# A two-layer hybrid mixer step on one core: early column groups cut into steps of two chunks, x scaled ahead, GpSimd relieved of a power and of transfers

## The chip, the cores and the metric

The kernel runs on one core of a Trainium2 chip. The metric is the device time of one execution in microseconds, of which the median over several runs is given. The engines are named as the profile names them: PE (matrix products; PEld loads its weights), DVE (vector), ACT (scalar functions), POOL (GpSimd) and SP (the engine that issues most transfers).

## The reference

The reference is one step of a network with two layers over 128 context tokens and 256 latent tokens, each a vector of 2048 numbers. A layer makes a shift, a scale and a gate from a conditioning vector (one for each kind of token), normalises the tokens, projects them to 7184 columns, runs four branches on the columns, and projects back:

```python
mod = jax.nn.silu(cond) @ lp['ada_w'] + lp['ada_b']
shift, scale, gate = jnp.split(mod, 3, axis=-1)
xm = rmsnorm(x, lp['norm_w']) * (1.0 + scale) + shift
pr = split_projection(xm @ lp['w_in'])
...
y = jnp.concatenate([out_a, out_b, out_c, out_d], axis=-1) @ lp['w_out']
x = x + gate * y
```

`out_a` is a gated linear recurrence in both directions, `out_b` a neighbourhood attention, `out_c` a grouped-query attention whose queries and keys are divided by their root mean square per head (`rmsnorm(pr['gqa_q'], ...)`) and rotated, and `out_d` a matrix memory (mLSTM). A last `rmsnorm` follows both layers. Besides the tokens, the new keys, values and branch states are written out.

## The kernel before

Tokens lie along the free axis: `xh[k]` and `xl[k]`, k from 0 to 15, hold chunk k of the modulated input, 128 features by 384 tokens (T), as a high and a low part, which together keep fp32 precision. A weight step loads two chunks' rows of up to 512 columns (`raw`), ACT rounds them to `wh`, POOL subtracts to get `wl` (`w_split`), and PE adds three products per chunk and block of output (`block`, the matmuls of line 1361): high by high, high by low, low by high. Blocks of 128 columns are numbered `nb`.

The modulation matrix `ada_w` is far larger than what PE could take beside its own work, so DVE computes it. `ada_dve` queues, for each half `s` of the matrix columns that serves two chunks, 16 rows of pieces: each piece multiplies a 128x512 tile (`araw`) by a condition and adds it to a sum in PSUM (`sbp`; line 196 as seen through the helper `stt`). Two transposes and two reductions (line 347, tile `red`) close the half. Then `ada_final` has PE pick the row sums (line 301, a matmul called the **selector** below), and a few small DVE operations put shift and scale for chunks 2s and 2s+1 into `mod` and `Amul`. Half 0 is made by PE at the start (`ada_pe`). Halves 8 to 11 are the gate. A selector stands in PE's queue at a fixed place: PE does nothing behind it until DVE has finished the half.

With shift and scale there, `modulate` makes `xh` and `xl` of a chunk: a product on DVE (`xmt`), a rounding with the shift on ACT (`xh`), the remainder on DVE (`xl`), each for the 128 context and the 256 latent tokens apart.

So that PE can start before all halves are there, the first layer visits nine column ranges (`E0`: `vif` to `gqa_k`, 4112 columns) in groups of chunks. `KG[0]` gives the chunks of each group: the plan runs all nine ranges over the group, then the next group. Between groups, the sum of a range is parked in SBUF: for `nb` 0 to 2 ACT copies it back to PSUM and out again (`PREB`), for `nb` 3 DVE adds. The late ranges (`ml_gate`, `na_k` and so on) run over all 16 chunks once. `merge` and the `due` list spread the pieces between weight steps. The lists give the order in which the code is written; the framework then sets each engine's queue, which is fixed when the kernel runs.

In the attention branch `br_gqa`, ACT sums the squares of 18 heads, POOL raises them to the power -1/2 (line 981), and DVE multiplies queries and keys (line 196), after which POOL issues the transfer of the keys (line 988) and DVE rotates them (lines 999 to 1004). PE transposes the result (line 1012), and ACT copies it to `gqT` and `gkT`.

Of the kernel before, what the change touches and what calls it, by code (L numbers as in the profile page):

```python
# [9 lines left out]
F32 = mybir.dt.float32  # L10
F32R = mybir.dt.float32r
# [66 lines left out]
def tile_hybrid_step(ctx: ExitStack, tc: tile.TileContext, I, O):  # L78
# [18 lines left out]
    E0 = ["vif", "ml_q", "ml_k", "ml_o", "lru_gate", "ml_v", "lru_x", "na_q", "gqa_k"]  # L97
    L0 = ["ml_gate"]
    NCRIT = 4
    SPREAD_AT, NPART = 2, 3  # L100
    YS = (4.0, 2.5, 1.0, 0.1)
    PRE = {0: True, 1: False}
    KG = {0: [2, 2, 2, 2, 4, 4], 1: [8, 8]}
    START = "PxPPxPPxPPxrPDDwwDD"
# [324 lines left out]
    def modulate(l, k, segs=((0, 0, TP), (1, TP, T))):  # L429
        if l == 0:  # L430
            x = xr[k]
        elif k < KG[1][0]:
            x = X[:, k, :]
        else:
            xr[k] = big.tile([128, T], F32, name=f"xr{k}", tag=f"xl{k}", bufs=1)
            if k < 14:
                nc.sync.dma_start(xr[k], xdram[:, k, :])
                x = xr[k]
            else:
                nc.sync.dma_start(xr[k].rearrange("p (t n) -> p t n", t=3), xtmd[:, :, (k - 14) * 128:(k - 13) * 128])  # L440
                x = from_tm(k)
        t = wrk.tile([128, T], F32, name="xmt", tag="t15", bufs=4)
        for c, a, b in segs:
            stt(t[:, a:b], x[:, a:b], Amul[:, l, k, c:c + 1], rbc[:, a:b], OP.mult, OP.mult)
        for c, a, b in segs:
            act(xh[k][:, a:b], t[:, a:b], AF.Identity, bias=mod[:, l, k, c:c + 1])
        if l == 0 or KG[1][0] <= k:
            xl[k] = big.tile([128, T], F32R, name=f"xl{k}", tag=f"xl{k}", bufs=1)
        for c, a, b in segs:
            stt(xl[k][:, a:b], t[:, a:b], mod[:, l, k, c:c + 1], xh[k].bitcast(F32)[:, a:b],  # L450
                OP.add, OP.subtract)

    def split_cat(k):
# [73 lines left out]
    def lru_alloc(key):  # L527
        t = six(key)
        v = lru_pad(t)
        nc.gpsimd.memset(v[:, :, 0:1], 0.0)  # L530
        nc.gpsimd.memset(v[:, :, 129:132], 0.0)
        nc.gpsimd.memset(v[:, :, 388:390], 0.0)
        return t

# [24 lines left out]
    kv_get = lazy("gqa_kv", lambda t: t[:, 0:1536].rearrange("p (s t n) -> p s t n", s=2, t=3), six)  # L559
    if_get = lazy("ml_if", lambda t: t, lambda key: wts.tile([128, 3, 16], F32, name="ml_if", tag="ml_if", bufs=1))  # L560
    gv_get = lazy("gqa_v", lambda t: t, lambda key: wts.tile([128, 3, 256], F32, name="gqa_v", tag="gqa_v", bufs=1))

# [67 lines left out]
    def br_mlstm(l):  # L630
# [33 lines left out]
        for h in range(4):  # L664
# [123 lines left out]
            yield 1.0  # L788
        nc.gpsimd.dma_start(O["mm"][l:l + 1, :], mnew)


    def br_lru(l):
# [29 lines left out]
        for g in range(4):  # L822
# [45 lines left out]
            yield 4.0  # L868
        nc.gpsimd.dma_start(O["lru"][l], lout)

# [92 lines left out]
    def br_gqa(l):  # L963
# [13 lines left out]
        for t in range(3):  # L977
            for ap, i, _ in heads(t):
                act(junk, ap, AF.Square, accum=ss[:, i:i + 1])
        nc.vector.tensor_scalar(ss, ss, 1.0 / 128, EPS, op0=OP.mult, op1=OP.add)  # L980
        nc.gpsimd.tensor_tensor(ss, ss, rpow[:, 0:18], op=OP.pow)  # L981
        ssq = ss.rearrange("p (t h) -> p t h", t=3)[:, :, 0:4]
        nc.vector.tensor_scalar(ssq, ssq, SC, None, op0=OP.mult)
        yield 8.0
        for t in range(3):
            for ap, i, wn in heads(t):
                stt(ap, ap, ss[:, i:i + 1], wn, OP.mult, OP.mult)
        nc.gpsimd.dma_start(O["gqa_k"][l], kk[:, 0, :])
        yield 2.0
        for t in range(2):  # L990
            cos = gqk[:, t * 128:(t + 1) * 128]
            sin = gqk[:, 256 + t * 128:256 + (t + 1) * 128]
            for ap, nh, wi in ((gq[:, 1 + t, :], 4, 0), (kk[:, 1 + t, :], 2, 1)):
# [10 lines left out]
                nc.vector.tensor_add(ap, ap, rot)  # L1004
            yield 4.0
        qT = cm(six("gqT"))
        kT = cm(six("gkT"))
# [48 lines left out]
    def lru_pairs(nb, ps):  # L1056
        return [(lru_get()[:, nb, 1:129], ps[:, 0:TP]), (lru_get()[:, nb, 132:388], ps[:, TP:T])]

    G = {
        "vif": tm_group([("gqa_v", 256), ("ml_if", 16)],  # L1060
                        lambda nb, ps: [(gv_get()[:, nb, :], ps[:, 0:256]), (if_get()[:, nb, :], ps[:, 256:272])]),
        "ml_q": cm_group("ml_q", lazy("ml_q", lambda t: t, lambda key: cat[:, 8:12, :]), SC),
# [3 lines left out]
                         start(br_mlstm)),  # L1066
        "lru_x": ("cm", [("lru_x", 512)], lru_pairs, copy_out(lru_pairs, 1.0, start(br_lru))),
        "na_q": cm_group("na_q", lazy("na_q", cm, six), SC),
# [104 lines left out]
    for l in range(DEPTH):  # L1173
# [6 lines left out]
        for i in range(len(KG[l])):  # L1180
            if i:
                side += ada_ss(l, kb[i], kb[i + 1]) + [mod_item(l, kb[i], kb[i + 1])]
                due.append((len(main) - LAG, len(side)))
            main += visits(l, EARLY[l], kb[i], kb[i + 1])
        m = o = 0
# [322 lines left out]
    for tok in START:  # L1508
# [5 lines left out]
        elif tok == "w":  # L1514
            upto("w", wl, w_dma, pos["w"] + 1)
        elif tok == "r":
            rstd_bc()
        elif tok == "P":
            it = first.pop(0)
            a_dma(it)  # L1520
            ada_pe(it)
        elif tok == "D":
            it = a_items[pos["a"]]
            upto("a", a_items, a_dma, pos["a"] + 1)
            ada_dve(it)
            it["early"] = True
# [154 lines left out]
```

## Time and profile before

| what | value |
|---|---|
| median of 3 runs | 1498.09 us (1495.1 to 1500.49) |
| the profiled execution | 1499.25 us |
| its span from first to last instruction | 1497.5 us |
| mean granted clock of PE | 0.975 |
| PE, DVE, ACT, POOL busy | 1411.3, 1083.7, 791.6, 922.0 us |

The profile is of one execution. Between its span and its time lie 1.75 us outside the instructions. A busy share is an average over stages: what an edit is worth is read from the stage in which it lies.

### The profile page before, as it was taken

To read this page: it belongs to the slowest core of one execution; us is meant where nothing else is said; L and a number is where in the kernel's file an instruction comes from. 1 tells how busy PE (TensorE), PEld (TensorE's weight loads), DVE (VectorE), ACT (ScalarE), POOL (GpSimd) and SP (SyncE) were. 2 spreads that over 40 slices of the span, in tenths; PEclk is the share of its full clock that TensorE was granted. 3 is DMA by queue.
4 is the path that set the end of the run, shared out by engine and by line. 5 is a ranking of instruction groups with operands and counts; after the bars stand their busy time and mean duration, and the time that the engine had idled before them with its cause. 6 is when DMAs were issued, how large, how long until landed. Compare 5 with 4: busy or idle time off the path is not lost. (4 is left out here: it accounts for less than half of the span.)

```text
span 1497.5 us, 23805 instructions
## 1 busy us (share of the span) xinstructions
PE 1411.3 (94%) x7999; PEld 1329.8 (89%) x7999; DVE 1083.7 (72%) x2053; ACT 791.6 (53%) x1609; POOL 922.0 (62%) x1230
## 2 busy tenths in 40 slices
PE   5989959999999899799998999999999999899997
PEld 1989949989998799799998999999999879899997
DVE  4989999989699956675658999646749761753533
ACT  4689936656445767353334334333454777463432
POOL 1656627666656774845646665766566875855762
PEclk8999979999999999999999999999999999999999
DMA  8877768776568555465747887655456444355433
GB/s 282 265 245 228 230 190 246 228 214 196 155 186 269 163 145 155 160 199 175 259 129 248 267 256 225 180 152 149 142 154 205 142 143 120 97 195 169 139 125 97
DMA packets 167164, 281.68 MB, mean 188 GB/s; under 512 B 17216, under 2 KB 48960, under 8 KB 166912
## 3 DMA queue, kind: packets, MB, share of 16 engines
q1 hardware_dynamic: 159520, 272.40, 59.6%
q10 hardware_dynamic: 7296, 7.48, 1.5%
q8 instruction: 62, 1.02, 0.3%
q14 instruction: 62, 0.51, 0.1%
q0 software_dynamic: 224, 0.27, 0.1%
HBM read 271.17 MB, written 8.93 MB: 187 GB/s over the span
## 5 line engine op out<-in xcount | busy, mean ns | idle before, releaser
L1243 POOL TENSOR_TENSOR wl<-raw,wh 128x256 fp32r<-128x256 f32 (+1 forms) x1152 | 874.5, 792 | 525.8 <-ACT wh L192 440.5
L1361 PE MATMUL acc<-xh,wh 128*128 128x384 f32 x1636 | 568.3, 348 | 15.4 <-ACT xh L192 7.0
L1361 PE MATMUL acc<-xh,wl 128*128 128x384 f32 x1636 | 553.0, 338 | 3.5 <-POOL wl L1243 3.5
L1361 PE MATMUL acc<-xl,wh 128*128 128x384 f32 x1636 | 555.0, 339 | 0.0
L196 DVE SCALAR_TENSOR_TENSOR sbp<-araw,pers,sbp 128x512 f32<-128x512 f32 x690 | 518.4, 751 | 20.9 <-DMA araw<-in_ada_n 8.1
L192 ACT ACTIVATE wh<-raw 128x1024 fp32r<-128x1024 f32 (+2 forms) x304 | 307.0, 1012 | 345.6 <-PE acc L1361 254.8
L1361 PEld LDWEIGHTS acc<-xh,wh 128*128 128x128 f32 x1636 | 309.3, 189 | 21.7 <-ACT xh L192 7.6
L1361 PEld LDWEIGHTS acc<-xh,wl 128*128 128x128 f32 x1636 | 309.2, 189 | 4.8 <-POOL wl L1243 4.8
L1361 PEld LDWEIGHTS acc<-xl,wh 128*128 128x128 f32 x1636 | 309.6, 189 | 1.4
L1361 PE MATMUL acc<-wh,xl 128*128 128x512 f32 (+2 forms) x454 | 166.6, 367 | 5.8 <-DVE xl L196 4.5
L1361 PE MATMUL acc<-wh,xh 128*128 128x512 f32 (+2 forms) x454 | 162.7, 359 | 0.0
L1361 PE MATMUL acc<-wl,xh 128*128 128x512 f32 (+2 forms) x454 | 161.7, 357 | 0.0
L1361 PEld LDWEIGHTS acc<-wh,xl 128*128 128x128 f32 x454 | 87.4, 193 | 21.8 <-DVE xl L196 7.8
L1361 PEld LDWEIGHTS acc<-wl,xh 128*128 128x128 f32 x454 | 87.2, 192 | 12.8
L1361 PEld LDWEIGHTS acc<-wh,xh 128*128 128x128 f32 x454 | 87.5, 193 | 10.9
L196 DVE SCALAR_TENSOR_TENSOR cat<-acc,pers,xold 128x128 f32<-128x128 f32 (+1 forms) x56 | 20.5, 410 | 65.7 <-PE acc L1361 65.7
L192 ACT ACTIVATE xh<-xmt,pers 128x128 fp32r<-128x128 f32 x72 | 29.4, 430 | 43.0 <-DVE xmt L196 42.9
L192 ACT ACTIVATE cat<-acc 128x384 f32<-128x384 f32 (+1 forms) x78 | 38.1, 498 | 8.8 <-PE acc L1361 7.8
L196 DVE SCALAR_TENSOR_TENSOR xl<-xmt,pers,xh 128x128 fp32r<-128x128 f32 x72 | 39.4, 567 | 2.1 <-ACT xh L192 1.9
L388 DVE TENSOR_TENSOR arena<-arena,sq 128x384 f32<-128x384 f32 x38 | 25.9, 682 | 17.4 <-ACT sq L192 16.0
L1361 PE MATMUL s<-xh,wh 128*128 128x384 f32 x92 | 32.2, 350 | 4.4 <-ACT xh L192 3.7
L192 ACT ACTIVATE xh<-cat 128x384 fp32r<-128x384 f32 x32 | 16.5, 519 | 37.1 <-PE acc L1361 19.6
(339 smaller groups left out, 1778.1 us busy)
## 6 DMA issues: line engine op xcount, KB each, us to landing
raw<-in_w_in SPq DMA_DIRECT2D x208, 512.0 KB, 4.0
araw<-in_ada_n SPq DMA_DIRECT2D x368, 256.0 KB, 4.3
raw<-in_w_out SPq DMA_DIRECT2D x64, 512.0 KB, 4.0
raw<-in_w_in SPq DMA_DIRECT2D x32, 256.0 KB, 3.1
araw<-in_ada_n SPq DMA_DIRECT2D x8, 512.0 KB, 5.3
xr<-in_xT SPq DMA_DIRECT2D x16, 192.0 KB, 5.2
nac<-in_nac SPq DMA_DIRECT2D x8, 288.0 KB, 4.4
xold<-in_xT SPq DMA_DIRECT2D x3, 768.0 KB, 6.1
```

The costliest lines, as they stand in the source:

```text
L192: return nc.scalar.activation(out, in_, f, bias=bias, scale=scale)
L196: return nc.vector.scalar_tensor_tensor(out, a, s, b, op0=op0, op1=op1)
L388: eng.tensor_tensor(sqacc, sqacc, s, op=OP.add)
L1243: nc.gpsimd.tensor_tensor(it["lo"][:, kk, cs], raw[:, kk, cs], hv[:, kk, cs], op=OP.subtract)
L1361: last_ev["pe"] = nc.tensor.matmul(out, a, b, start=s0 and i == 0, stop=s1 and i == 2, skip_group_check=not it["first"]).ins
```

## The change

`KG[0]` goes from groups of 2, 2, 2, 2, 4 and 4 chunks to eight groups of 2, with one exception: the four ranges of `LAST4` skip the seventh group and take chunks 12 to 15 in one visit in the eighth. In the first layer x is multiplied by 1/rms in place beforehand (`unit_rms`): six chunks on DVE as soon as 1/rms is known, ten chunks on POOL. `modulate0` then has ACT make `xh` from x directly, with scale and shift, and DVE make the unrounded value with one two-scalar operation and `xl` with one subtraction over all tokens. The parked sums of `lru_x` are kept without the gaps that the convolution needs (384 wide in one piece; `lru_out` puts the gaps in at the end), and those of `vif` in one tile of 272 columns. In `br_gqa`, 1/rms comes from ACT's square root and one Newton step on DVE (`rms_newton`: a reciprocal and three small operations) instead of POOL's power. The transfers of `mm`, `lru` and `gqa_k` go from POOL's queue to ACT's. The power in `br_mlstm` (line 772) stays on POOL.

```diff
+    LAST4 = ("lru_gate", "lru_x", "na_q", "gqa_k")
...
-    KG = {0: [2, 2, 2, 2, 4, 4], 1: [8, 8]}
+    KG = {0: [2, 2, 2, 2, 2, 2, 2, 2], 1: [8, 8]}
...
     def modulate(l, k, segs=((0, 0, TP), (1, TP, T))):
         if l == 0:
-            x = xr[k]
-        elif k < KG[1][0]:
+            modulate0(k)
+            return
+        if k < KG[1][0]:
...
+    def unit_rms(k, eng):
+        for a in (0, TP) if eng is nc.gpsimd else (0,):
+            b = T if a or eng is nc.vector else TP
+            eng.tensor_tensor(xr[k][:, a:b], xr[k][:, a:b], rbc[:, a:b], op=OP.mult)
+
+    def modulate0(k):
+        x = xr[k]
+        t = wrk.tile([128, T], F32, name="xmt", tag="t15", bufs=4)
+        for c, (a, b) in enumerate(SEG):
+            act(xh[k][:, a:b], x[:, a:b], AF.Identity, bias=mod[:, 0, k, c:c + 1], scale=Amul[:, 0, k, c:c + 1])
+        for c, (a, b) in enumerate(SEG):
+            nc.vector.tensor_scalar(t[:, a:b], x[:, a:b], Amul[:, 0, k, c:c + 1], mod[:, 0, k, c:c + 1],
+                                    op0=OP.mult, op1=OP.add)
+        xl[k] = big.tile([128, T], F32R, name=f"xl{k}", tag=f"xl{k}", bufs=1)
+        nc.vector.tensor_sub(xl[k], t, xh[k].bitcast(F32))
+        if 6 <= k + 4 < KC:
+            unit_rms(k + 4, nc.gpsimd)
...
+    def lru_out(l, nb, ps, summed):
+        v = lru_get()
+        src = ps
+        if not summed:
+            src = wrk.tile([128, T], F32, name="lrus", tag="t15", bufs=4)
+            nc.vector.tensor_add(src, ps[:, :T], v[:, nb, 1:385])
+        act(v[:, nb, 1:129], src[:, 0:TP], AF.Copy)
+        act(v[:, nb, 132:388], src[:, TP:T], AF.Copy)
+        if nb == 3:
+            for a, b in ((0, 1), (129, 132), (388, 390)):
+                nc.gpsimd.memset(v[:, :, a:b], 0.0)
+            start(br_lru)(l)
...
-        nc.gpsimd.dma_start(O["mm"][l:l + 1, :], mnew)
+        defer(4.0, lambda: nc.scalar.dma_start(O["mm"][l:l + 1, :], mnew))
...
-        nc.gpsimd.dma_start(O["lru"][l], lout)
+        defer(6.0, lambda: nc.scalar.dma_start(O["lru"][l], lout))
...
+        root = slot("uv")[:, 0:18]
+        act(root, ss, AF.Sqrt, bias=epsc, scale=1.0 / 128)
         nc.vector.tensor_scalar(ss, ss, 1.0 / 128, EPS, op0=OP.mult, op1=OP.add)
-        nc.gpsimd.tensor_tensor(ss, ss, rpow[:, 0:18], op=OP.pow)
+        rms_newton(root, ss, slot("uv")[:, 32:50])
+        nc.vector.tensor_copy(ss, root)
...
-        nc.gpsimd.dma_start(O["gqa_k"][l], kk[:, 0, :])
         yield 2.0
...
+        nc.scalar.dma_start(O["gqa_k"][l], kk[:, 0, :])
         qT = cm(six("gqT"))
...
-            main += visits(l, EARLY[l], kb[i], kb[i + 1])
+            for name in EARLY[l]:
+                if l == 0 and name in LAST4 and i >= 6:
+                    if i == 7:
+                        main += visit(l, name, kb[6], kb[8])
+                else:
+                    main += visit(l, name, kb[i], kb[i + 1])
...
         elif tok == "r":
             rstd_bc()
+            for k in range(6):
+                unit_rms(k, nc.vector)
```

The first place is PE's queue at the selector of half 5, which opens chunks 10 and 11. Before, it stands in the middle of the first two chunks of the group of four (`xl_2136` and `xl_2153` are chunks 8 and 9, `xl_2170` is chunk 10):

```order
L1361 MATMUL s_79<-wh,xl_2153 128x272
L1361 MATMUL s_79<-wh,xh 128x272
L1361 MATMUL s_79<-wl,xh 128x272
L1361 MATMUL acc_112<-xl_2153,wh 128x384
L1361 MATMUL acc_112<-xh,wl 128x384
L301 MATMUL s_80<-red,pers 128x32
L1361 MATMUL s_80<-xh,wh 128x384
L1361 MATMUL s_80<-xl_2136,wh 128x384
```

After the change it stands in `ml_v` (512 columns) of the group of chunks 8 and 9, which are `xl_1767` and `xl_1802` here:

```order
L1402 MATMUL acc_114<-wh,xl_1767 128x512
L1402 MATMUL acc_114<-wh,xh 128x512
L1402 MATMUL acc_114<-wl,xh 128x512
L302 MATMUL s_80<-red,pers 128x32
L1402 MATMUL acc_114<-wh,xl_1802 128x512
L1402 MATMUL acc_114<-wh,xh 128x512
L1402 MATMUL acc_114<-wl,xh 128x512
L1402 MATMUL s_80<-xh,wh 128x384
```

Between the selectors of halves 4 and 5 there are 105 matmuls of this line in the order of before, and 195 in that of the change.

The second place is POOL's queue at the start. Before, the remainders `wl` of the weights come first:

```order
L1243 ISA
L1243 TENSOR_TENSOR wl<-raw,wh 128x272 x2
L1243 TENSOR_TENSOR wl<-raw,wh 128x256 x30
```

After it, products of x with 1/rms (`xr_96` is chunk 6) stand ahead of the first `wl` and between the next ones; these rows go on in the same way to `xr_105`:

```order
L458 ISA
L458 TENSOR_TENSOR xr_96<-xr_96,pers 128x128
L458 TENSOR_TENSOR xr_96<-xr_96,pers 128x256
...
L458 TENSOR_TENSOR xr_100<-xr_100,pers 128x128
L1284 TENSOR_TENSOR wl<-raw,wh 128x272 x2
L458 TENSOR_TENSOR xr_100<-xr_100,pers 128x256
L458 TENSOR_TENSOR xr_101<-xr_101,pers 128x128
L458 TENSOR_TENSOR xr_101<-xr_101,pers 128x256
L1284 TENSOR_TENSOR wl<-raw,wh 128x256 x4
```

Nine products stand ahead of the first `wl`, three more ahead of the next four, and eight more ahead of the rest.

The third place is POOL's queue in `br_gqa` of the first layer. Before:

```order
L869 DMA out_lru<-arena 128x8
L1243 TENSOR_TENSOR wl<-raw,wh 128x256 x36
L981 TENSOR_TENSOR arena<-arena,pers 128x18
L988 DMA out_gqa_k<-gqa_k 128x256
L1243 TENSOR_TENSOR wl<-raw,wh 128x256 x52
```

After, nothing but `wl` is left between the last memset of `br_lru` and the next layer:

```order
L833 MEMSET xc 128x1
L1284 TENSOR_TENSOR wl<-raw,wh 128x256 x96
L565 MEMSET ml_v 128x12
```

The power, and the transfer that waits for DVE's keys, no longer stand between the weight remainders.

## Rows read from the trace of the kernel before

**Rows 1.** The page, part 1: busy time, share and count by engine.

```profile
PE 1411.3 (94%) x7999; PEld 1329.8 (89%) x7999; DVE 1083.7 (72%) x2053; ACT 791.6 (53%) x1609; POOL 922.0 (62%) x1230
```

**Rows 2.** Windows: stretch, its length, busy us (and count) by engine, clock, DMA.

```profile
core 0: us, PE busy (x) PEld busy (x) DVE busy (x) ACT busy (x) POOL busy (x), PEclk, DMA share, GB/s
...
85.00:195.00 110.00, 106.79 (x614) 101.13 (x612) 101.94 (x171) 99.86 (x235) 68.30 (x94) 1.00 0.77 231
195.00:215.00 20.00, 3.93 (x12) 3.32 (x13) 19.44 (x35) 1.04 (x3) 2.77 (x4) 0.56 0.63 200
...
310.00:430.00 120.00, 118.22 (x709) 114.06 (x708) 98.31 (x204) 63.61 (x153) 69.81 (x93) 0.99 0.62 178
```

**Rows 3.** Waits of PE, whole span: in total, times, longest.

```profile
PE s L301 <- DVE red L347: 16.3, 5, 13.3
```

**Rows 4.** Timeline of PE, the selectors of halves 4, 5, 8, 9, 10.

```profile
175.11 0.30 PE L301 MATMUL acc<-red,pers 128*128 128x32 f32 x2
...
208.15 0.42 PE L301 MATMUL s<-red,pers 128*128 128x32 f32 x1 [13.34 <-DVE red L347]
...
309.36 0.30 PE L301 MATMUL s<-red,pers 128*128 128x32 f32 x1 [1.79 <-DVE red L347]
...
367.37 0.30 PE L301 MATMUL s<-red,pers 128*128 128x32 f32 x2
...
431.80 0.30 PE L301 MATMUL s<-red,pers 128*128 128x32 f32 x2
```

**Rows 5.** Timeline of DVE, the last reduction of halves 9 and 10.

```profile
362.84 0.67 DVE L347 TENSOR_REDUCE red<-turned 128x16 f32<-128x512 f32 x1
...
425.00 0.67 DVE L347 TENSOR_REDUCE red<-turned 128x16 f32<-128x512 f32 x1
```

**Rows 6.** DVE by line and shape, 33 to 310 us: busy, mean ns, idle before.

```profile
L196 DVE SCALAR_TENSOR_TENSOR sbp<-araw,pers,sbp 128x512 f32<-128x512 f32 x239 | 179.6, 751 | 4.3
...
L196 DVE SCALAR_TENSOR_TENSOR xl<-xmt,pers,xh 128x256 fp32r<-128x256 f32 x16 | 10.7, 671 | 0.1
...
L196 DVE SCALAR_TENSOR_TENSOR xmt<-xr,pers 128x256 f32<-128x256 f32 x16 | 10.2, 635 | 0.0
...
L196 DVE SCALAR_TENSOR_TENSOR xmt<-xr,pers 128x128 f32<-128x128 f32 x16 | 9.1, 569 | 0.1
L196 DVE SCALAR_TENSOR_TENSOR xl<-xmt,pers,xh 128x128 fp32r<-128x128 f32 x16 | 7.7, 478 | 0.0
```

**Rows 7.** Lines 721 and 455: durations, least/median/most ns, first and last start.

```profile
L721 DVE TENSOR_SCALAR arena<-ml_v,u x16: 268/270/766, 340.3 to 1131.5; 128x129 f32<-128x129 f32 x16
L455 DVE TENSOR_TENSOR xl<-cat,xh x32: 528/560/1140, 582.5 to 1373.7; 128x384 fp32r<-128x384 f32 x32
```

**Rows 8.** Timeline, start: ACT copies 1/rms; DVE's first step on half 0.

```profile
29.82 0.49 ACT L192 ACTIVATE pers<-s 128x384 f32<-128x384 f32 x1 [2.37 <-PE s L408]
...
32.88 0.23 DVE L285 COPY pers<-s 128x4 f32<-128x4 f32 x2 [2.32 <-PE s L283]
```

**Rows 9.** Timeline of POOL, 592 to 615 us.

```profile
593.35 3.50 POOL L981 TENSOR_TENSOR arena<-arena,pers 128x18 f32<-128x18 f32 x1
599.38 0.60 POOL L988 DMA_DIRECT2D out_gqa_k<-gqa_k  x1 [2.53 <-DVE gqa_k L196]
600.01 15.60 POOL L1243 TENSOR_TENSOR wl<-raw,wh 128x256 fp32r<-128x256 f32 x8
```

**Rows 10.** Timeline of PE at its stalls around `br_gqa`, both layers.

```profile
613.28 0.45 PE L1361 MATMUL acc<-xh,wl 128*128 128x384 f32 x1 [1.67 <-POOL wl L1243]
...
622.12 0.47 PE L1012 MATMUL s<-pers,cat 128*128 128x128 f32 x1 [5.53 <-ACT gqT L192]
...
1295.14 0.69 PE L1361 MATMUL acc<-xh,wh 128*128 128x384 f32 x1 [4.21 <-DVE gth L196]
```

**Rows 11.** Lines by shape: ACT's table loads; the page, part 5: `wl`.

```profile
L192 ACT ACT_TABLE_LOAD x22 | 28.2, 1283 | 11.8 <-DVE arena L858 9.7 <-PEq L1658 1.2 <-DVE pers L202 0.6
...
L1243 POOL TENSOR_TENSOR wl<-raw,wh 128x256 fp32r<-128x256 f32 (+1 forms) x1152 | 874.5, 792 | 525.8 <-ACT wh L192 440.5
```

More of the change, by code (lines that the diff above doesn't have):

```diff
@@ L446, in modulate @@
             act(xh[k][:, a:b], t[:, a:b], AF.Identity, bias=mod[:, l, k, c:c + 1])
-        if l == 0 or KG[1][0] <= k:
+        if KG[1][0] <= k:
             xl[k] = big.tile([128, T], F32R, name=f"xl{k}", tag=f"xl{k}", bufs=1)
@@ L527, in lru_alloc @@
     def lru_alloc(key):
[L528 to L533, printed above, removed]
+        return six(key)
+    def lru_out(l, nb, ps, summed):
[10 more added lines that the diff above has]
+            start(br_lru)(l)
     def mlv_alloc(key):
@@ L559, in tile_hybrid_step, with vif_alloc @@
     kv_get = lazy("gqa_kv", lambda t: t[:, 0:1536].rearrange("p (s t n) -> p s t n", s=2, t=3), six)
-    if_get = lazy("ml_if", lambda t: t, lambda key: wts.tile([128, 3, 16], F32, name="ml_if", tag="ml_if", bufs=1))
-    gv_get = lazy("gqa_v", lambda t: t, lambda key: wts.tile([128, 3, 256], F32, name="gqa_v", tag="gqa_v", bufs=1))
+    def vif_alloc(key):
+        t = wts.tile([128, 3, 272], F32, name="vif", tag="vif", bufs=1)
+        S["gqa_v"], S["ml_if"] = t[:, :, 0:256], t[:, :, 256:272]
+        return t
+    vif_get = lazy("vif", lambda t: t, vif_alloc)
     def mlo(l, nb, ps, summed):
@@ L1056, in lru_pairs @@
     def lru_pairs(nb, ps):
-        return [(lru_get()[:, nb, 1:129], ps[:, 0:TP]), (lru_get()[:, nb, 132:388], ps[:, TP:T])]
+        return [(lru_get()[:, nb, 1:385], ps[:, 0:T])]
     G = {
         "vif": tm_group([("gqa_v", 256), ("ml_if", 16)],
-                        lambda nb, ps: [(gv_get()[:, nb, :], ps[:, 0:256]), (if_get()[:, nb, :], ps[:, 256:272])]),
+                        lambda nb, ps: [(vif_get()[:, nb, :], ps[:, 0:272])]),
         "ml_q": cm_group("ml_q", lazy("ml_q", lambda t: t, lambda key: cat[:, 8:12, :]), SC),
@@ L1066, in tile_hybrid_step @@
                          start(br_mlstm)),
-        "lru_x": ("cm", [("lru_x", 512)], lru_pairs, copy_out(lru_pairs, 1.0, start(br_lru))),
+        "lru_x": ("cm", [("lru_x", 512)], lru_pairs, lru_out),
         "na_q": cm_group("na_q", lazy("na_q", cm, six), SC),
```

## The prediction

> **What bounds the kernel now.** I read the shares first: PE is busy for 94% of the span [rows 1], so a gain must come out of the 86 us in which it is not, or out of stretches at the lower clock. Then the windows [rows 2]. From 85 to 195 us PE runs almost without a gap, and DVE is busy for 101.9 of 110 us as well. From 195 to 215 PE works for 3.9 of 20 us at a granted clock of 0.56, while DVE is busy for 19.4: PE waits for DVE. The waits of PE name it: the selector waits for `red`, 16.3 us in all and 13.3 in one piece [rows 3]. The timeline of the selectors [rows 4] shows that piece at 208.15, where half 5 is finished: the group of four chunks needs halves 4 and 5, and PE runs out of work on what half 4 opened. The reader is to see two more things there. Half 8 makes PE wait 1.79 us, halves 9 and 10 don't. And DVE finishes half 9 at 363.5 and half 10 at 425.7 [rows 5], 3.9 and 6.1 us before PE asks: the next limit is close behind.
>
> **Part 1, groups of two.** PE's matmuls between selectors, counted in the two orders: before, 105 between halves 4 and 5, then 143, 173, 212, 276 and 288 up to half 10; after, 195, 193, 176, 188, 193 and 267. A matmul takes 0.179 us (110 us by 614, [rows 2]). So from half 4 at 175.1 PE would ask for half 5 at 175.1 + 34.9 = 210.0, where DVE has had it ready at 208: the wait of 13.3 goes. Half 8 would be asked for at 210.0 + (193 + 176 + 188) x 0.179 = 309.7, where DVE has it at 309.3. In the new order the first matmul on half 7's chunks stands only 12 places behind its selector, 2.1 us, while DVE's small operations and ACT's rounding lie between; I take a wait of 3.5 us there (an estimate), and PE is at half 8 at about 313. To half 9 PE took 58.0 us for 276 matmuls, branch work included, 0.210 each; 193 of them make 40.5, so it asks at 353.7. Here DVE is late: before it had half 9 at 363.5. In 310 to 430 DVE was idle for 21.7 of 120 us [rows 2], part of it waiting for PE and ACT, and such idle time shrinks when DVE is the one that is late. I take 361, two to three us of it won back, and to half 10 another 267 x 0.224 (64.4 us by 288) = 59.7, which is 420.7 for PE and about 423 with DVE. Before, PE came to the same place (12 matmuls behind its half 10) at 431.8 + 2.7 = 434.5. The gain is 11.5 us; half 11 has slack, so it stays.
>
> **Part 2, DVE's work.** The supply of halves is a sum of DVE's rows. A piece is 0.751 us, 32 to a half [rows 6], and is unchanged. Added: six products of 128x384 before half 0. No such row stands there; the nearest, the subtraction of line 455, takes 0.56 us alone and 1.14 at most [rows 7], so 3.4 to 6.8; I take 5.4, since POOL does the like at the same time. Removed and added per chunk: 0.569 + 0.635 + 0.478 + 0.671 = 2.35 us [rows 6] become two `tensor_scalar` and one subtraction: at least 0.27 + 0.36 + 0.56 = 1.2 (0.27 is 129 columns of line 721 [rows 7], 0.36 scaled from it and the subtraction for 256), at most 0.77 + 0.77 + 1.14 = 2.7. Nearest are rows of the same operations between these ends, so 1.95: 16 x 0.4 = 6.4 less, with ends of 18.4 less and 5.6 more. Extra visits add to parked sums for `nb` 3: two for each of `ml_q`, `ml_k` and `ml_o`, one for `lru_gate` and `na_q`, four fewer for `lru_x` in one piece: 4 x 0.56 = 2.2 more. Sum 5.4 - 6.4 + 2.2 = +1.2 us up to half 8, ends -12.8 and +14.6. The +1.2 is in part 1's 361 and 423.
>
> Both sides of this sum hang on company. A row shows one `tensor_scalar` of 129 columns at 0.268 or at 0.766 us [rows 7], and eight `wl` in 15.6 us [rows 9] against 0.792 each on average [rows 11], while DVE multiplies queries and keys. A rule speaks against the change here: the Trainium skill, Advanced Engine Details and Errata, Mode Summary, says that DVE's second SBUF port is shared with GpSimd, so that two-port DVE instructions and GpSimd's block each other; the trace agrees. By that rule alone every new `tensor_scalar` would sit at its upper end, and the sum of this part would be about +8 us.
>
> **Part 3, the start.** 1/rms is in SBUF at 30.31, and DVE is idle for 2.32 us up to 32.88 [rows 8]. The six products fill that and end 3.1 us later than 32.88; PE's first matmul then no longer waits for a product on DVE (`xmt`, 0.57 [rows 6]). On POOL nine products stand ahead of the first `wl`: at 0.79 for 256 columns and somewhat less for 128 about 6 us, and eleven more among the next. PE starts perhaps 2.5 us later and waits 1 to 2 us for `wl`. This costs nothing further, since PE then meets halves 5 to 9 with as much more slack, and DVE's delay is in part 2; without that cover it is 4 us.
>
> **Part 4, `br_gqa`.** In the first layer POOL spends 3.50 us on the power, waits 2.53 for DVE's keys and 0.60 on the transfer [rows 9], 6.6 us, then does eight `wl` in 15.6 us. What is late next is `wl` (PE 1.67), then ACT, which holds the next rounding until a buffer is free, and with it `gqT` (PE 5.53) [rows 10]. All of it hangs on POOL, so PE gets most of 6.6 us back, against it an ACT table load of 1.28 us there and one back [rows 11]. DVE's chain stays as long: five small operations and one load for a power of 3.5. I take 6, ends 0 and 9 (with the matmuls at the lower clock behind the stall). In the second layer the stall of 4.21 is ended by DVE's `gth`, behind its run of multiplications, which starts about when it did: 1.5, ends -1 and 4. Sum 7.5.
>
> **The rest at nothing.** Fewer copies for `vif` and `lru_x`, and more visits, are ACT's: 99.9 us of 110 in the fullest stretch [rows 2] with PE not waiting for them; uncovered, the two per block saved would be some 2 us a group. The transfers of `mm` and `lru` leave a POOL that idles; the early stretch moves the same bytes at a DMA share of 0.77.
>
> **Sum.** 11.5 + 7.5 = 19 less on the profiled 1499.25 makes 1480.25; that execution lies 1.2 us above the median of the runs, from which it would be 1479.1. I leave 1.5 for the part of PE's later start that is not covered: 1481. New queues in the branches can move waits of one to four us either way.
>
> **The rivals.** *DVE keeps up* (chance 0.16): if the modulation sits at its lower end and idle time is won back in full, PE meets no wait at halves 9 and 10, and is at 353.7 + 59.7 = 413.4 at half 10, 21 us ahead; with 7.5 that is 1471. For it speaks the idle 21.7 us, against it DVE at 93% already from 85 to 195 us [rows 2]. *The gain is given back* (0.17): the waits only move from half 5 to halves 8 to 10, because DVE's rate is what it was, and the branches wait for DVE behind; about 2 us stay, `br_gqa` gives 4.5: 1492.5. *Slower* (0.09): DVE and POOL hold each other up. If the new operations are at their upper ends, +14.6, half 10 is done at 440.3, 5.8 us later than PE came to the same place before; the point is 434.5 - 425.7 = 8.8 us of added DVE work. With half of part 4 lost to the added DVE chain and table loads (about 1.5 left) it gives 1503. The rule on the shared port, above, is this rival at its worst. *Nothing* (0.08): the queues change, both stalls come back in other places, 1498.
>
> **How the numbers follow.** The forecast, 1481 with a range of its own of 1474 to 1489, has 0.50. A measurement of this kernel tells about 0.3%, 4.5 us, from no change. Faster: 0.50 + 0.16 + 0.12 of the third case = 0.78. Same: the other 0.05 of it and the 0.08 of nothing = 0.13. Slower: 0.09. The range reaches from 1468, into the first rival, to 1497, past the third case, and leaves out the last two.
>
> **What would show it.** PE's wait at the selector of half 5 under 3 us; the window 195 to 215 at full clock; halves 8 and 9 with new waits of 2 to 8 us; eight `wl` behind the keys' products without the gap, and the stalls at `gqT` and `wl` under 3 us together. It is wrong if the selectors' waits add up to 16 us again, if DVE's `xmt` and `xl` come out above 2.35 us a chunk, or if PE waits more for ACT than for DVE in the groups from chunk 8 on.

## The result and the profile after

The changed kernel took 1476.5 us (median of 5 runs, 1474.54 to 1480.24), the kernel before 1495.1 on the same chip (1494.1 to 1500.49). The ratio is 0.9866, 95% interval 0.9845 to 0.9887: 1.3% less time. Measured once more on another occasion, the same code came to 0.9818 (0.9801 to 0.9834). The two intervals don't touch; experiment 5 asks why, and explains a part of it. The profiled execution took 1480.24 us, its span is 1478.4.

PE is now busy for 96% of the span. The page, part 1, answers to [rows 1]:

```profile
PE 1415.2 (96%) x7999; PEld 1331.2 (90%) x7999; DVE 1080.4 (73%) x2050; ACT 828.1 (56%) x1638; POOL 914.5 (62%) x1242
```

The windows of [rows 2], after:

```profile
core 0: us, PE busy (x) PEld busy (x) DVE busy (x) ACT busy (x) POOL busy (x), PEclk, DMA share, GB/s
85.00:195.00 110.00, 108.74 (x626) 104.78 (x627) 99.63 (x171) 100.51 (x211) 68.31 (x95) 0.98 0.78 235
195.00:215.00 20.00, 20.00 (x112) 19.18 (x111) 17.62 (x31) 18.63 (x37) 10.77 (x16) 1.00 0.82 252
310.00:430.00 120.00, 116.51 (x698) 111.05 (x697) 110.69 (x232) 62.28 (x154) 68.74 (x93) 0.99 0.68 200
...
278.00:292.00 14.00, 9.99 (x44) 8.72 (x45) 13.04 (x27) 8.56 (x17) 9.12 (x13) 0.76 0.58 166
```

In 195 to 215 PE works without a gap at full clock, where it worked for 3.93 of 20 us. A new thin place is at 278 to 292: 9.99 of 14 us, clock 0.76 (0.50, the lower of the clock's two levels, from 281.6 to 288.4). PE's timeline shows what it is; the selectors (L302) of halves 4, 5, 7, 8, 9 and 10 answer to [rows 4], the last two rows are the places of `br_gqa` in [rows 10]:

```profile
178.05 0.30 PE L302 MATMUL s<-red,pers 128*128 128x32 f32 x2
...
211.79 0.30 PE L302 MATMUL s<-red,pers 128*128 128x32 f32 x2
...
278.90 0.41 PE L302 MATMUL acc<-red,pers 128*128 128x32 f32 x2 [1.21 <-DVE red L348]
279.65 0.44 PE L1402 MATMUL acc<-xh,wh 128*128 128x384 f32 x1 [0.34 <-DVE picked L305]
282.48 0.69 PE L1402 MATMUL acc<-xh,wh 128*128 128x384 f32 x1 [1.50 <-DVE lru_x L1371]
285.29 0.59 PE L1402 MATMUL acc<-wh,xl 128*128 128x272 f32 x1 [0.53 <-DVE xl L469]
...
319.58 0.41 PE L302 MATMUL s<-red,pers 128*128 128x32 f32 x2 [0.29 <-DVE red L348]
...
363.76 0.30 PE L302 MATMUL s<-red,pers 128*128 128x32 f32 x2
...
424.47 0.30 PE L302 MATMUL s<-red,pers 128*128 128x32 f32 x2
...
600.50 0.66 PE L1048 MATMUL s<-pers,cat 128*128 128x128 f32 x4 [0.44 <-DVE cat L1039]
...
1275.78 0.69 PE L1402 MATMUL acc<-xh,wh 128*128 128x384 f32 x1 [6.99 <-DVE gth L197]
```

The selector of half 5 doesn't wait. Behind half 7, four short waits add up to 3.58 us. Halves 9 and 10 don't wait. The stalls of the first layer's `br_gqa` (1.67 and 5.53) are down to 0.44; the one of the second layer has grown from 4.21 to 6.99. There `gth` is DVE's product of a gate with a sum of PE's, and PE's next product waits for it.

To see where the time went, I numbered the 6,912 matmuls of the main products (line 1361 and the tail's line 1402 before; 1402 and 1443 after) in the order of their starts, and took the start in the kernel before less that in the other, number by number. Up to about number 2,000 the groups differ in order, so there the number means about equal amounts of work (the columns differ most at number 1300, by what takes about 1.5 us, an estimate from 0.179 us a matmul); behind it the work is the same matmul for matmul. The table holds this lead in us, for the changed kernel and for all experiments. In the changed order numbers 800 to 1000 hold half 5 and 1000 to 1300 halves 6 and 7, and the early groups end at number 1583. Number 1926 stands right behind half 10 in the changed order and 12 matmuls behind it in that of before: it is the place for which the prediction gives the gain of the groups. Numbers 2600 to 2700 hold `br_gqa` of the first layer, 5900 to 6000 that of the second.

```
number            0    800   1000   1300   1700   1926   2600   2700   5900   6000    end
changed        -2.1   -3.6   19.4   10.8    9.4    9.2   12.5   23.1   22.1   18.8   18.7
again           0.4   -1.7   21.3   12.7   11.6   11.5   14.1   24.7   26.2   31.6   31.6
p_groups       -1.0   -2.4   18.4    6.5    2.9    3.3    6.1    7.2    8.8    8.4    8.5
p_mod          -3.0   -7.5   -4.2   -4.1   -2.4   -2.4   -0.6   -0.3    0.3    0.3    0.7
p_gqa          -0.4    0.2    0.2    0.2    1.2    0.6    0.8   11.2   11.8   17.2   17.2
p_rest          0.0   -1.0   -1.0   -0.5   -3.6   -4.1   -4.6   -4.7   -3.5   -4.1   -4.1
u_mod           0.3    0.5   22.2   10.3    5.3    4.0    3.9   14.5   15.3   20.8   20.7
u_rest         -1.7   -4.9   17.7    7.9    7.8    7.0    9.4   20.0   20.8   26.1   26.5
l1_order       -1.3   -3.2   19.8   11.2   10.0    9.7   13.8   24.4   26.0   25.6   25.5
pow_back       -1.2   -3.6   19.5   11.0   10.5   10.2   13.6   20.4   21.0   20.6   20.6
dma_back       -1.8   -3.5   19.6   11.0   10.3   10.0   13.3   15.6   15.6   21.0   21.0
hold            0.5   -2.0   21.0   12.4   11.2   10.9   14.3   24.9   26.7   28.7   28.7
hold_late       2.5   -0.8   22.2   13.4   12.2   12.1   15.5   26.1   26.9   29.0   28.9
```

So the changed kernel is 9.2 us ahead behind half 10 and 12.5 just ahead of the first `br_gqa`, gains 10.6 there, and loses 3.3 at the second. The rows `changed` and `again` are the same code and lie 1.6 to 2.5 us apart up to number 2700, so a difference of 2 us between two rows there says little by itself.

### The profile page after: what moved, and what is told of

The parts are those of the page before. It is cut to its first block, busy times and chain, and to the rows that moved or that the text cites. A ratio compares the mean times of both kernels' runs of the same rounds, so it can differ in the third digit from the quotient of the medians.

```text
span 1478.4 us, 23865 instructions
## 1 busy us (share of the span) xinstructions
PE 1415.2 (96%) x7999; PEld 1331.2 (90%) x7999; DVE 1080.4 (73%) x2050; ACT 828.1 (56%) x1638; POOL 914.5 (62%) x1242
## 5 line engine op out<-in xcount | busy, mean ns | idle before, releaser
L1284 POOL TENSOR_TENSOR wl<-raw,wh 128x256 fp32r<-128x256 f32 (+1 forms) x1152 | 864.9, 785 | 477.5 <-ACT wh L193 414.3
L197 DVE SCALAR_TENSOR_TENSOR sbp<-araw,pers,sbp 128x512 f32<-128x512 f32 x690 | 517.6, 750 | 27.2 <-DMA araw<-in_ada_n 15.6
L1402 PEld LDWEIGHTS acc<-xh,wh 128*128 128x128 f32 x1630 | 309.0, 190 | 25.7 <-ACT xh L193 10.4
L1402 PEld LDWEIGHTS acc<-wl,xh 128*128 128x128 f32 x452 | 88.0, 195 | 12.5
L193 ACT ACTIVATE cat<-acc 128x384 f32<-128x384 f32 (+1 forms) x94 | 46.2, 495 | 5.4 <-PE acc L1402 4.8
L334 DVE TENSOR_SCALAR sbp<-araw,pers 128x512 f32<-128x512 f32 x46 | 34.3, 745 | 0.2
```

Of the source, the lines that this page charges most:

```text
L193: return nc.scalar.activation(out, in_, f, bias=bias, scale=scale)
L197: return nc.vector.scalar_tensor_tensor(out, a, s, b, op0=op0, op1=op1)
L334: d = nc.vector.tensor_scalar(acc, raw, sc, None, op0=OP.mult)
L1284: nc.gpsimd.tensor_tensor(it["lo"][:, kk, cs], raw[:, kk, cs], hv[:, kk, cs], op=OP.subtract)
L1402: last_ev["pe"] = nc.tensor.matmul(out, a, b, start=s0 and i == 0, stop=s1 and i == 2, skip_group_check=not it["first"]).ins
```

## The experiments

Theory: the early gain is the wait of half 5, which goes because the groups of two put more matmuls ahead of it; the gain of `br_gqa` is POOL's time for power and transfer. Rivals: the early gain is the relief of DVE by the shorter modulation; the gain of `br_gqa` comes from its place having shifted.

**1. The groups alone (p_groups).**

```diff
-    KG = {0: [2, 2, 2, 2, 4, 4], 1: [8, 8]}
+    KG = {0: [2, 2, 2, 2, 2, 2, 2, 2], 1: [8, 8]}
+    LAST4 = ("lru_gate", "lru_x", "na_q", "gqa_k")
...
+                if l == 0 and name in LAST4 and i >= 6:
+                    if i == 7:
+                        main += visit(l, name, kb[6], kb[8])
```

> The kernel before with the groups of two chunks and the four late groups in fours, nothing else. Theory (the wait goes): the wait of 13.3 us at the selector of half 5 goes whatever DVE's work is, because more matmuls stand ahead of it; 7 to 12 us less than before (ratio 0.992 to 0.995), no wait over 3 us at halves 4 to 8. Rival (the relief of DVE): the groups pay only because the shorter modulation lets DVE keep up; then the waits move to halves 8, 9 and 10 (together over 8 us) and the time is 0 to 4 us less.

Measured: 1488.14 us against 1497.51, ratio 0.9942 (0.9927 to 0.9958), 8.7 us by the ratio. PE's timeline:

```profile
212.28 0.30 PE L302 MATMUL s<-red,pers 128*128 128x32 f32 x2
...
281.94 0.41 PE L302 MATMUL acc<-red,pers 128*128 128x32 f32 x2 [1.19 <-DVE red L348]
...
288.26 0.59 PE L1367 MATMUL acc<-wh,xl 128*128 128x272 f32 x1 [4.25 <-DVE xl L197]
...
365.90 0.33 PE L781 MATMUL s<-pers,arena 128*128 128x128 f32 x1 [3.17 <-DVE xc L197]
```

The wait of half 5 is gone without any relief of DVE. But the lead falls from 18.4 to 2.9 between numbers 1000 and 1700: PE waits 4.25 us for `xl` behind half 7, and 3.17 for `xc` of a branch. PE's waits between these numbers add up to 12.5 us, where the kernel before has 2.7, and from 284.9 to 291.7 the clock is 0.50. The time is in the theory's range, but its waits of at most 3 us are not, and the lead of 6.1 at number 2600 is near the rival's 0 to 4, though the waits stand behind half 7 and in a branch, not at halves 8 to 10. Both carry a part.

**2. The modulation alone, and everything but the modulation (p_mod, u_mod).**

```diff
 elif tok == "r":
     rstd_bc()
+    for k in range(6):
+        unit_rms(k, nc.vector)
```

with `modulate0` and its products on GpSimd (p_mod); u_mod takes the same lines out of the changed kernel.

> The kernel before with x scaled by 1/rms ahead and the new modulation, groups as before. Theory: the six products delay PE's first matmul by 2 us and DVE's supply by about 4, the shorter modulation gives 0.6 us a chunk back, half 5 still stops PE for 10 to 15 us; 4 us less to 3 us more than before. Rival (the relief of DVE is the gain): the wait at half 5 shrinks to under 8 us and the time is 6 to 11 us less.

> The changed kernel with the old modulation (no products with 1/rms ahead). Theory (the shorter modulation matters only together with groups of two, where DVE is late at halves 7 to 10): PE starts 2 to 3 us earlier, but waits 4 to 8 us more for DVE from half 7 on; 2 to 7 us slower than the changed kernel. Rival (the two cancel, as they do in the kernel before): within 1.5 us of it.

Measured: alone 1496.01, ratio 0.9991 (0.9979 to 1.0003), no difference. The changed kernel without it: 1477.95, ratio 0.9882 (0.9862 to 0.9902) where the changed kernel of the same occasion has 0.9818: 9.2 us slower, more than the 2 to 7 expected. PE of p_mod, then of u_mod:

```profile
212.09 0.64 PE L301 MATMUL s<-red,pers 128*128 128x32 f32 x2 [11.96 <-DVE red L347]
```

```profile
278.63 0.64 PE L302 MATMUL acc<-red,pers 128*128 128x32 f32 x2 [3.58 <-DVE red L348]
...
363.69 0.43 PE L794 MATMUL s<-pers,arena 128*128 128x128 f32 x1 [4.16 <-ACT arena L193]
```

In the old groups half 5 stops PE for 11.96 us with the new modulation, 13.34 with the old. In groups of two half 7 comes 3.58 us late without it instead of 1.21, the clock behind it is 0.50 for 13.7 us (278.4 to 292.1) instead of 6.8, a branch's operand comes 4.16 us late, and the lead at number 2600 is 3.9, not 14.1. The edit pays nothing alone and about 9 us together with the groups.

**3. The smaller edits alone, and everything but them (p_rest, u_rest).** Unpadded sums of `lru_x`, the merged `vif` tile, the transfers of `mm` and `lru`.

```diff
-        return [(lru_get()[:, nb, 1:129], ps[:, 0:TP]), (lru_get()[:, nb, 132:388], ps[:, TP:T])]
+        return [(lru_get()[:, nb, 1:385], ps[:, 0:T])]
...
-        nc.gpsimd.dma_start(O["lru"][l], lout)
+        defer(6.0, lambda: nc.scalar.dma_start(O["lru"][l], lout))
```

> The kernel before with the unpadded partial sums of lru_x, the merged vif tile and the two deferred transfers, nothing else. Theory: within 2 us of before. Rival (ACT's copies or the transfers were on the path): 4 us or more less.

> The changed kernel with the old padded partial sums of lru_x, the old vif tiles, and the mm and lru transfers on GpSimd in their old places. Theory (these edits cost in the old grouping only, by an ACT wait at gqa_k near 360 us that the new grouping does not have): within 2 us of the changed kernel. Rival (they cost as much here as alone, 4 to 5 us): 1471 to 1473, ratio about 0.983.

Measured: alone 1502.6, ratio 1.0036 (1.0022 to 1.005), 0.4% more time, a miss; everything but them 1472.65, ratio 0.9843 (0.9826 to 0.9859) against 0.9818, so that here they are worth 3.7 us by the ratios. These intervals overlap, the single times (1470.86 to 1473.1 against 1467.42 to 1469.5) don't. That fits neither the theory (within 2 us) nor the rival (a gain without them): the time falls into the rival's 1471 to 1473 only because the changed kernel itself took 1468.76 on this occasion. PE of p_rest (before, the same wait is 0.52 us, at 359.08), then of u_rest:

```profile
361.33 0.45 PE L1374 MATMUL acc<-xh,wh 128*128 128x384 f32 x1 [2.37 <-ACT gqa_k L192]
```

```profile
287.11 0.59 PE L1389 MATMUL acc<-wh,xl 128*128 128x272 f32 x1 [4.49 <-DVE xl L469]
```

Alone they make ACT late with the last copies of `gqa_k`, a loss that the new groups don't have; it is 1.85 of the 3.1 us lost between numbers 1300 and 1700. With the new groups the wait of 4.49 us takes the place of several: with 0.40 and 0.34 ahead of it, PE waits 5.23 us behind half 7, the changed kernel 3.58 (3.90 in `again`). That is 1.3 to 1.7 us, and at number 1000, ahead of it, the lead is already 1.7 to 3.6 us smaller. So the cause of the 3.7 us isn't shown. Which of the three edits does it wasn't tried.

**4. `br_gqa` alone, and its two halves undone (p_gqa, pow_back, dma_back).**

```diff
-        nc.gpsimd.tensor_tensor(ss, ss, rpow[:, 0:18], op=OP.pow)
+        rms_newton(root, ss, slot("uv")[:, 32:50])
...
-        nc.gpsimd.dma_start(O["gqa_k"][l], kk[:, 0, :])
...
+        nc.scalar.dma_start(O["gqa_k"][l], kk[:, 0, :])
```

p_gqa has all of it on the kernel before; pow_back and dma_back take the first or the second piece out of the changed kernel.

> The kernel before with the new br_gqa alone (root on ACT, Newton steps on DVE, transfer later and from ACT's queue). Theory: the first layer gains 9 to 11 us by the stalls at wl and gqT, the second loses 2 to 4, since POOL's splits and DVE's multiplications now run at the same time there; 6 to 8 us less. Rival (the shift of the early part did it): without the earlier end of the early groups the branch stands elsewhere against the weights and the gain is under 3 us; then also no loss in the second layer.

> The changed kernel with the power back on GpSimd in br_gqa of both layers (root on ACT and Newton steps on DVE go), the gqa_k transfer stays late and on ACT's queue. Theory (POOL's 3.5 us of power and 3.1 us of transfer with its wait each carry their share of the 10.6 us that the first layer gained): 3 to 6 us of it are lost at the first layer's br_gqa, stalls at wl and gqT of 2 to 5 us together. Rival A (the transfer's wait was all of it): under 1.5 us lost. Rival B (the power was all of it): over 8 us lost.

> The changed kernel with the gqa_k transfer back on GpSimd, between the multiplications and the rotations, in both layers; root and Newton steps as changed. Theory: 3 to 6 us lost at the first layer's br_gqa, since POOL waits for the keys' products and starts its splits later. Rival A (the power was all of it): under 1.5 us lost. Rival B (the transfer's wait was all of it): over 8 us lost. In the second layer, theory (a POOL that waits for DVE's products can't slow them): the run of DVE up to the rotations takes its undisturbed 4.7 us.

Measured: alone 1481.78, ratio 0.9894 (0.9878 to 0.9911), 15.9 us, twice what I expected: 10.4 at the first layer, as expected, but a gain of 5.4 at the second, where I expected a loss. With the power back 1478.77, ratio 0.9883 (0.9869 to 0.9898); with the transfer back 1477.57, 0.9873 (0.9858 to 0.9889). At the first layer the gain is 10.6 us in every trace with the new groups and both pieces. Without the first piece 3.8 of it go, inside the theory's 3 to 6; without the second 8.3, which is the size of rival B. Together that is more than the whole, so the two overlap. PE of pow_back, then of dma_back, POOL of dma_back, and at last POOL of the changed kernel:

```profile
602.48 0.93 PE L1045 MATMUL s<-pers,cat 128*128 128x128 f32 x6 [2.32 <-ACT gqT L193]
```

```profile
600.76 0.45 PE L1402 MATMUL acc<-xh,wl 128*128 128x384 f32 x1 [1.94 <-POOL wl L1284]
...
608.94 1.54 PE L1048 MATMUL s<-pers,cat 128*128 128x128 f32 x6 [3.84 <-ACT gqT L193]
```

```profile
588.65 0.75 POOL L1024 DMA_DIRECT2D out_gqa_k<-gqa_k  x1 [2.65 <-DVE gqa_k L197]
589.43 20.52 POOL L1284 TENSOR_TENSOR wl<-raw,wh 128x256 fp32r<-128x256 f32 x16
```

```profile
587.22 2.93 POOL L1284 TENSOR_TENSOR wl<-raw,wh 128x256 fp32r<-128x256 f32 x4 [0.37 <-ACT wh L193]
592.71 13.35 POOL L1284 TENSOR_TENSOR wl<-raw,wh 128x256 fp32r<-128x256 f32 x6 [2.57 <-ACT wh L193]
```

The transfer costs POOL 3.4 us (2.65 of waiting, 0.75 of its own) and the branch 8.3. In the changed kernel POOL does four splits in 2.93 us beside DVE's multiplications, while with the transfer it waits there, and these splits too fall into DVE's rotations, beside which POOL is slow in both kernels (six in 13.35 us). At the second layer dma_back did as expected: DVE's multiplications take 4.8 us, and the branch gains 5.4.

**5. The second layer: the same code again (again).** No edit.

> The changed kernel once more. Question: in the profiled execution DVE's run of multiplications in br_gqa of the second layer took 15.5 us against POOL's splits (9.4 us with the same instructions where the new br_gqa stands alone). Theory (which of the two engines gives way is a matter of their phase, and of the execution): here the run takes 9 to 16 us and the time moves with it, PE's wait for gth under 2 us when it takes under 11. Rival (the shift of the branch fixes it): again 15 to 16 us, PE's wait 6 to 8 us. Time: 1476 to 1480, ratio 0.985 to 0.989.

Measured: 1468.76 (1467.42 to 1469.5), ratio 0.9818, below the expected 1476 to 1480; DVE's run took 9.4 us, PE's wait 0.91, and the branch gained 5.4 us instead of losing 3.3. That is 8.7 of the 12.8 us between the two profiled executions; 1.6 lie ahead of the first `br_gqa`, 2.5 between the two. DVE's timeline in the first profile of the changed kernel and in this one, the same instructions, with `gth` at the end:

```profile
1259.98 1.13 DVE L197 SCALAR_TENSOR_TENSOR cat<-cat,arena,gqk 128x128 f32<-128x128 f32 x4
1261.04 0.35 DVE L197 SCALAR_TENSOR_TENSOR gqa_k<-gqa_k,arena,gqk 128x128 f32<-128x128 f32 x1
1261.30 2.58 DVE L197 SCALAR_TENSOR_TENSOR cat<-cat,arena,gqk 128x128 f32<-128x128 f32 x4
...
1267.37 0.95 DVE L1034 TENSOR_TENSOR arena<-cat,gqk 128x256 f32<-128x256 f32 x1
...
1275.18 0.54 DVE L197 SCALAR_TENSOR_TENSOR gth<-gth,acc 128x384 f32<-128x384 f32 x1
```

```profile
1255.98 1.14 DVE L197 SCALAR_TENSOR_TENSOR cat<-cat,arena,gqk 128x128 f32<-128x128 f32 x4
1257.03 0.35 DVE L197 SCALAR_TENSOR_TENSOR gqa_k<-gqa_k,arena,gqk 128x128 f32<-128x128 f32 x1
1257.29 1.14 DVE L197 SCALAR_TENSOR_TENSOR cat<-cat,arena,gqk 128x128 f32<-128x128 f32 x4
...
1260.44 0.42 DVE L1034 TENSOR_TENSOR arena<-cat,gqk 128x256 f32<-128x256 f32 x1
...
1265.07 0.55 DVE L197 SCALAR_TENSOR_TENSOR gth<-gth,acc 128x384 f32<-128x384 f32 x1
```

And POOL's timeline in the same two executions:

```profile
1261.40 3.08 POOL L1284 TENSOR_TENSOR wl<-raw,wh 128x256 fp32r<-128x256 f32 x4 [2.46 <-ACT wh L193]
1265.62 3.28 POOL L1284 TENSOR_TENSOR wl<-raw,wh 128x256 fp32r<-128x256 f32 x4 [1.14 <-PE acc L1402]
1269.84 3.80 POOL L1284 TENSOR_TENSOR wl<-raw,wh 128x256 fp32r<-128x256 f32 x4 [0.93 <-ACT wh L193]
```

```profile
1257.38 8.36 POOL L1284 TENSOR_TENSOR wl<-raw,wh 128x256 fp32r<-128x256 f32 x1 [2.46 <-ACT wh L193]
```

In both POOL's split starts 1.7 us into DVE's run. In the first it gets through, in 3 to 4 us for four, and DVE's four multiplications take 2.58 instead of 1.14. In the second one split of about 0.73 us lasts 8.36, until DVE's run ends, and DVE isn't slowed. So the two engines stand in each other's way, and the price is 15.5 us against 9.4 for DVE's run (from its first multiplication to `gth`). The Trainium skill, Advanced Engine Details and Errata, Mode Summary, says that GpSimd and two-port DVE instructions block each other at a shared SBUF port. Both executions agree that the two engines block each other; whether DVE's instructions here are two-port ones they don't show, and which engine gives way that section doesn't say: here either did.

What decides it the traces don't show. The phase, which the theory names, doesn't, as far as they resolve it: in the first profile of the changed kernel and in again, p_gqa, u_mod, u_rest and l1_order POOL's split starts 1.67 or 1.68 us after DVE's first multiplication, and in all but the first POOL gives way. Of the twelve traces without the hold of experiment 7, the kernel before among them, eleven have DVE's 18 multiplications in 4.8 us, and only that first profile has them in 7.7. The other four executions of the first occasion have no trace. They lie 5 us and more above all of this one, but also 3.6 to 5.7 below the profiled one, so what happened in them is open. The three occasions of the experiments were on three chips (the kernel before took 1497.51, 1495.45 and 1495.72 there), that of the first result isn't known, and a part of the chip in the difference isn't excluded.

**6. The second layer: `gth` ahead of the rotations (l1_order).**

```diff
+            gates.extend(traced(lambda: stt(th, th, 1.0, ps[:, :T], OP.add, OP.mult)))
...
+                    for g in gates if l else ():
+                        if g.engine == mybir.EngineType.DVE:
+                            order(turn_.ins, g)
```

> The changed kernel with one ordering more: in the second layer DVE does the four gth before the rotations of br_gqa instead of behind them; nothing else, and POOL's splits stay where they are. Theory (PE waits for gth only because gth stands behind the run that POOL slows): the wait of 7.0 us goes to under 1.5 us, the stretch at half clock behind it goes too, 5 to 9 us less than the profiled changed kernel at the same matmul, 1468 to 1473. Rival (ACT's table loads and the longer chain set it): gth is not ready earlier, the wait stays over 4 us and the time within 2 us of the changed kernel.

Measured: 1473.78 (1470.36 to 1475.93), ratio 0.985 (0.9831 to 0.987). PE's wait for `gth` is gone, as the theory has it, but a stretch at a clock of 0.50 stays (1280.8 to 1287.6), and the branch as a whole still loses 0.4 us:

```profile
1281.95 1.11 PE L1051 MATMUL s<-pers,cat 128*128 128x128 f32 x4 [4.12 <-DVE cat L1042]
```

The rotations now run beside POOL's splits and the transposes wait for them. The time is 2.7 us below the first occasion of the changed kernel and 5.0 above the second, and its interval overlaps with both: the wait has moved.

**7. POOL held in the second layer, and a shorter start (hold, hold_late).**

```diff
+                if l and t and not wi:
+                    last_ev["hold"] = nc.gpsimd.tensor_copy(held1, ap[:, 0:1]).ins
...
+                if it["i"] == 265:
+                    order(low.ins, last_ev["hold"])
```

hold_late, besides: `range(2)` for `range(6)` at the start, the four other products ordered behind `xl` of chunk 1.

> The changed kernel, where in the second layer a one-column copy on GpSimd that reads DVE's last product of the queries holds POOL's next splits until DVE's run of br_gqa is over (the branch's pieces are handed out without pauses there, so that the copy stands ahead). Theory (the second layer is fast when DVE has its run to itself and POOL gives way, as in the execution with 9.4 us): DVE's run takes 9 to 10 us for certain, PE's wait for gth is under 2 us, the branch gains 4 to 6 us instead of losing 3, and the executions lie close together: 1466 to 1470. Rival (held splits come too late): PE waits 3 us or more for wl, 1472 or more.

> The kernel with POOL held, and at the start only the products of chunks 0 and 1 with 1/rms ahead of the modulation; those of chunks 2 to 5 stand behind xl of chunk 1 on DVE. Theory (PE's later start is covered, because half 7 is where DVE's supply decides): PE's first matmul comes 2 to 3 us earlier, and the lead is gone by half 8; within 1 us of the kernel with POOL held. Rival (the late start is paid to the end): 2 to 3 us less to the end.

Measured: held 1470.74 (1469.99 to 1471.89), ratio 0.9831 (0.9816 to 0.9845); with the shorter start 1471.13, 0.9833 (0.9818 to 0.9849). POOL, DVE and PE of the held kernel:

```profile
1264.66 0.31 POOL L1043 COPY pers<-cat 128x1 f32<-128x1 f32 x1 [10.29 <-DVE cat L1041]
```

```profile
1265.01 1.19 DVE L1044 TENSOR_TENSOR cat<-cat,arena 128x512 f32<-128x512 f32 x1
...
1267.00 0.54 DVE L197 SCALAR_TENSOR_TENSOR gth<-gth,acc 128x384 f32<-128x384 f32 x1
```

```profile
1266.26 0.55 PE L1059 MATMUL s<-pers,cat 128*128 128x128 f32 x3 [1.70 <-DVE cat L1044]
1267.59 0.69 PE L1415 MATMUL acc<-xh,wh 128*128 128x384 f32 x1 [0.78 <-DVE gth L197]
```

POOL idles 10.29 us and PE doesn't wait for `wl`. DVE has its multiplications to itself, and the copy starts 9.5 us after the first of them. But POOL's splits are then free while DVE still rotates (1.19 us for an addition that takes 0.69 in `again`), and the first `gth` comes 11.8 us after the first multiplication, not 9 to 10. The branch gains 2.0 us, less than the 4 to 6 expected: the transposes wait 1.70 us, `gth` 0.78. The interval of the held kernel ends at 0.9845, where that of the changed kernel's first occasion begins; from the second occasion (0.9818) it can't be told apart. The shorter start brings PE's first matmul 2.0 us earlier; 1.0 is left at number 1700, not gone by half 8 as expected, 0.2 at the end, and the times are the same: an earlier start gains nothing here.

## Why the prediction was right, and where not

**The time.** 1481 forecast, 1476.5 measured, in the range and in the likeliest case's own. The profiled execution came out at the 1480.25 of the sum, but by errors that cancel: 4.6 us too little for the first `br_gqa`, 4.8 too much for the second. It was the slowest of the five, so this agreement is luck. On the second occasion the same code took 1468.76, below the likeliest case's 1474 to 1489 and nearer to the first rival's 1471, though not by that rival's mechanism.

**Groups of two.** Forecast 11.5 behind half 10; measured there 9.2, and 11.5 in `again`. By number 2600 it is 12.5 and 14.1: between the two PE waits 5.7 us at matmuls of the branches before the change, 3.4 after it, which the prediction left out. The wait of half 5 went, with the selector at 211.79 for a forecast of 210.0. The wait of 3.5 us behind half 7 came as 3.58, in four pieces. What failed is the step that DVE is late at halves 9 and 10, and with it the sign of new waits of 2 to 8 us at halves 8 and 9. DVE's last reductions, answering to [rows 5]:

```profile
361.27 1.23 DVE L348 TENSOR_REDUCE red<-turned 128x16 f32<-128x512 f32 x2
...
415.74 1.24 DVE L348 TENSOR_REDUCE red<-turned 128x16 f32<-128x512 f32 x2
```

They end at 362.5 and 417.0, and PE asks at 363.76 and 424.47, near the 361 and 423 of the text, but without waiting. PE itself was late at half 8, which it asked for at 319.3, not 313, and waited for 0.29 us. The time went instead into half clock behind half 7 (278 to 292 at 0.76), which I hadn't counted, and into the branches: PE's waits between numbers 1000 and 1700 add up to 8.0 us (2.7 before), 2.3 of them for DVE's operand of a branch.

**DVE's work.** Forecast +1.2 us; the modulation's rows, answering to [rows 6], and the products:

```profile
L469 DVE TENSOR_TENSOR xl<-xmt,xh 128x384 fp32r<-128x384 f32 x16 | 11.3, 704 | 0.0
...
L466 DVE TENSOR_SCALAR xmt<-xr,pers 128x256 f32<-128x256 f32 x16 | 8.8, 549 | 0.0
L466 DVE TENSOR_SCALAR xmt<-xr,pers 128x128 f32<-128x128 f32 x16 | 8.4, 526 | 0.0
```

```profile
31.31 4.43 DVE L458 TENSOR_TENSOR xr<-xr,pers 128x384 f32<-128x384 f32 x6 [0.57 <-ACT pers L193]
```

A chunk takes 28.5 / 16 = 1.78 us (forecast 1.95, before 2.36) and the products 4.43 (5.4): with the 2.2 of the visits as forecast, which I didn't measure, 4.43 - 9.3 + 2.2 = -2.7. The price of +8, with every new `tensor_scalar` at its upper end of 0.77, didn't come: they took 0.549 and 0.526 on average. A small miss by size, but I treated this term as a correction of part 1. Experiments 1 and 2 show that it decides what of the groups' gain is kept: the lead at number 2600 is 3.9 without it and 14.1 with it on the same occasion.

**The start.** Forecast about 2.5 us later and covered. The two executions of the changed kernel start 2.1 us later and 0.4 earlier than that of the kernel before, so single executions don't settle the size. Experiment 7 shows that two us of an earlier start bring nothing at the end.

**First `br_gqa`.** The mechanism was right, the term mis-sized: 6 (ends 0 and 9) against 10.6. I took POOL's own 6.6 us; the transfer alone was worth 8.3, since what stands behind it falls into DVE's run. I had also put the slow `wl` of [rows 9] beside the multiplications alone; these end at 602.2, and most of the 15.6 us lie beside the rotations behind them.

**Second `br_gqa`.** Forecast 1.5 (ends -1 and 4); -3.3 and +5.4 were measured, both outside. The failed step is that DVE's run "starts about when it did" and so keeps its length. From DVE's first operation on the sums to the first multiplication it is 1.7 us now, 5.7 before, so that the run starts 2.3 to 2.4 us earlier against PE's work (the lead at number 5900 taken off), and how long the run lasts depends on POOL. The rival of DVE and POOL holding each other up took place there, at one spot and in one of two executions, not in the modulation.

**The rest at nothing.** Wrong alone (-4.1 at the end), worth some 3.7 with the groups, from a cause that stays open.

## What to carry to other kernels

Don't expect the parts of a change to add up: here one part was worth nothing alone and 9 us beside another, and one changed its sign. Whoever moves work off a shared engine should ask what that engine will run beside instead. Where two engines hold each other up, a true dependence can set which one gives way, but here it moved the wait and was no faster than the better of the two occasions. And measure on more than one occasion: one alone would have hidden that the second `br_gqa` can go either way.

## What was not expected of the hardware

One GpSimd subtraction of 128x256, 0.73 us alone, lasted 8.36 us while DVE ran `scalar_tensor_tensor` and `tensor_tensor` in SBUF back to back (in the kernel before, too, three take 9.76 us there); in another execution of the changed program it took 0.84 and DVE's run 15.5 us instead of 9.4. Two measurements of one program, each steady within 6 us, lay 0.5% apart.
